# Linear attention's output kept by pairs of heads, with norm, factors and gates of each pair applied by PSUM bank

## The chip, the cores and the metric

The program runs on one core of a Trainium2 chip. Its engines are TensorE (PE, matrix products and transposes), VectorE (DVE), ScalarE (ACT) and GpSimd (POOL); SyncE (SP) issues the DMAs. The metric is the device time of one execution in microseconds, as the median of several runs. One profiled execution gives the trace from which all rows here are read.

## The reference, cut to what matters

One step of a hybrid decoder layer over 2048 prompt tokens and 32 sample tokens, all in float32. What the change touches is the mixer's linear attention (GLA) and what follows it up to the output projection:

```python
q, k, v, r, a, u, sv = split_cols(xn @ w_in)
logg = log_sigmoid(a @ w_alpha + b_alpha) / GLA_TAU
o, S = gla_chunked(q, k, v, logg, s0)          # S_t = diag(alpha_t) S_{t-1} + k_t^T v_t ; o_t = q_t S_t
o = rmsnorm(o, g_gla_out)                      # over the 128 values of each of 4 heads
o = o.reshape(B, T, GLA_WIDTH) * silu(r)
s_out = gelu(u) * sgu_spatial(rmsnorm(gelu(sv)), w_s, b_s)
y = concatenate([o, s_out]) @ w_out
```

Behind the mixer come a cross attention over 256 memory tokens, a gated feed-forward network with a short convolution, and the final norm. The program has all of them; the change leaves them alone.

## The kernel before

The prompt is worked in four blocks of 512 tokens (0 to 3); block 1 also carries the 32 sample tokens, so that its tiles are 544 wide. Large products are made of three matmuls of rounded parts (`mm3`, lines 92 to 94): each weight is split into `h_` and `l_` parts, each activation too. One block runs the input projection (tiles `t_wv`, `a_wu`, `t_wr`, ...), the linear attention, the spatial gating unit (`zp`, `z`), the output projection (`a_wo`), attention and the feed-forward network.

The linear attention works pair by pair (p is 0 or 1, two of the four heads each). For a pair, seven levels build the causal products in P: `e` (difference of sums, VectorE; two exponentials, ScalarE; times k, VectorE), `kr` (two on VectorE), four matmuls `s` (line 1044) into one PSUM bank, and two predicated copies of it into P (line 1048). Then `decay` and `states`: VectorE's `kh` (line 1073), its exponential on ScalarE (1079), its product with k on GpSimd (1080), four transposes `ktp` (1083), the copy `kt`, products `kv`, and the chain of states S. `chunks(p, i)` makes one PSUM bank `op` of 512 columns: two chunks of 128 tokens, two heads each; its two halves are copied to 256 columns of the tiles `o[c]`, one for each chunk of 128 tokens and 512 wide over all four heads.

When both pairs are in `o`, the tail runs: `onorm(c)` for each chunk (square on ScalarE, sum by heads on VectorE, `rt` on VectorE and `ors` on GpSimd for the inverse root, `o` times `r` on VectorE), `gate(c)` (`o` times `ors`), then `back(h)` for each head: four transposes `otp` (line 1185), one for each chunk, and the split into `ch` and `cl` that the output projection multiplies with.

What sets the order: `weave` lists the steps with the main work (input and output projections) and says between which main steps the others start; the framework's scheduler then lays the instructions out for each engine when the program is built, and each engine runs its own list in order, waiting on semaphores. So a step that moves in the list also moves work of other engines. In block 0 two fold stages of weights (`vop`, `voh`, `vol`) are woven in as well. `h_wo`, `l_wo`, `h_wr`, `l_wr` are splits of weights that arrive by DMA: ScalarE writes the `h_` part and VectorE the `l_` part.

## Time and profile before

| | us |
|---|---|
| median of 3 runs (lowest, highest) | 2838.52 (2836.45, 2841.78) |
| the profiled execution | 2836.71 |
| its span, first to last instruction | 2835.0 |
| TensorE busy in the span | 2794.4 (99%) |
| VectorE, ScalarE, GpSimd busy | 1891.3, 1104.5, 575.5 |
| TensorE's mean granted clock | 0.996 of full speed |

A row of the trace gives the start of an instruction or of a run of like instructions from the span's start, how long it lasted, engine, line, operation and tiles; in brackets stands the idle time of that engine ahead of it and the instruction that ended it. Matmuls are pipelined, so a row of one lasts longer than the distance to the next, and rates are read from distances. The granted clock is 1.00 at 2.4 GHz and 0.50 at 1.2 GHz.

### The profile page before, as it was taken

The numbers are of one execution on the slowest core, as the hardware profiler recorded it, in microseconds if no ns is written. First come the engines' busy times: TensorE is split into PE (matmuls) and PEld (weight loads), VectorE is DVE, ScalarE is ACT, GpSimd is POOL, SyncE is SP. The second block draws the span as 40 slices with busy tenths as digits, with TensorE's granted clock in tenths as the row PEclk, the third lists the DMA queues.
The fourth block names the chain that finished last, engine by engine and source line by source line (L and its number), as shares of the span: only waits on it lengthen the run. The fifth ranks groups of instructions, "written<-read, shape, count | busy, mean of one in ns | idle before, by whom it ended". The sixth has DMA issues, their size and how long they took to land.

```text
span 2835.0 us, 47063 instructions
## 1 busy us (share of the span) xinstructions
PE 2794.4 (99%) x17894; PEld 2473.9 (87%) x17894; DVE 1891.3 (67%) x3266; ACT 1104.5 (39%) x1950; POOL 575.5 (20%) x638
## 2 busy tenths in 40 slices
PE   8999999999999999999999999999999999999998
PEld 8888888888888898898888889899999888899997
DVE  6578778777657776655555777766666677665555
ACT  5645544333363354222124445422223545421222
POOL 2002212111111221222220121222221022132222
PEclk9999999999999999999999999999999999999999
DMA  9756589999932255888995226577776323577775
GB/s 306 244 182 219 188 273 340 335 339 333 328 109 77 83 164 196 309 290 290 324 340 169 82 61 208 196 260 256 258 264 215 102 70 133 201 260 273 271 282 177
DMA packets 369687, 638.21 MB, mean 225 GB/s; under 512 B 27370, under 2 KB 238412, under 8 KB 369462
## 3 DMA queue, kind: packets, MB, share of 16 engines
q1 hardware_dynamic: 369462, 635.20, 65.9%
q8 instruction: 142, 2.33, 0.3%
q14 instruction: 83, 0.68, 0.1%
HBM read 507.69 MB, written 127.41 MB: 224 GB/s over the span
## 4 chain that ended last, share of the span: by engine, by line
PE 61%; DVE 4%; ACT 1%; issue 1%; POOL 1%; DMA 0%; POOLq 0%; SPq 0%; DVEq 0%; ACTq 0%
PE d L94 4%; PE d L92 4%; PE d L93 4%; PE a_wx L94 1%; PE a_wx L93 1%; PE a_wx L92 1%; PE s L1044 1%; PE a_wo L92 1%; PE a_wo L93 1%; PE a_wu L92 1%; PE a_wu L93 1%; PE a_wo L94 1%; PE t_wr L92 1%; PE t_wr L93 1%; PE a_wu L94 1%
## 5 line engine op out<-in xcount | busy, mean ns | idle before, releaser
L92 PE MATMUL d<-acth,whi_wd 128*128 128x272 f32 (+1 forms) x688 | 235.3, 342 | 0.0
L94 PE MATMUL d<-acth,wlo_wd 128*128 128x272 f32 (+1 forms) x688 | 233.3, 340 | 0.0
L93 PE MATMUL d<-actl,whi_wd 128*128 128x272 f32 (+1 forms) x688 | 233.0, 339 | 0.0
L1679 DVE TENSOR_TENSOR h<-d,h 128x512 f32<-128x512 f32 (+1 forms) x232 | 133.5, 581 | 148.0 <-PE d L94 147.8
L1581 POOL TENSOR_TENSOR c<-c,bc_f 128x512 f32<-128x512 f32 (+1 forms) x88 | 139.3, 1589 | 134.2 <-ACT c L1580 133.4
L1571 ACT ACTIVATE c<-g,colsb 128x512 f32<-128x512 f32 x88 | 71.7, 815 | 202.9 <-DVE g L1540 152.7
L94 PEld LDWEIGHTS d<-acth,wlo_wd 128*128 128x128 f32 x688 | 129.3, 188 | 15.5 <-issue 1.2
L93 PEld LDWEIGHTS d<-actl,whi_wd 128*128 128x128 f32 x688 | 129.3, 188 | 13.6 <-issue 0.4
L92 PEld LDWEIGHTS d<-acth,whi_wd 128*128 128x128 f32 x688 | 129.5, 188 | 13.1
L1603 POOL TENSOR_TENSOR c<-r_q_wup,c 128x512 f32<-128x512 f32 (+1 forms) x33 | 63.0, 1908 | 337.7 <-DVE r_q_wup L286 215.9
L1568 POOL COPY carry<-g 128x2 f32<-128x2 f32 x88 | 30.6, 348 | 432.8 <-DVE g L1540 430.7
L92 PE MATMUL a_wo<-ch,h_wo 128*128 128x512 f32 (+1 forms) x320 | 113.2, 365 | 2.3 <-ACT r L874 1.5
L93 PE MATMUL a_wo<-cl,h_wo 128*128 128x512 f32 (+1 forms) x320 | 113.4, 357 | 0.0
L94 PE MATMUL a_wo<-ch,l_wo 128*128 128x512 f32 (+1 forms) x320 | 112.6, 355 | 0.0
L1572 DVE SCALAR_TENSOR_TENSOR c<-g,colsb,c 128x512 f32<-128x512 f32 x88 | 86.0, 978 | 29.0 <-ACT c L1571 28.3
L84 ACT ACTIVATE acth<-c 128x512 fp32r<-128x512 f32 (+1 forms) x88 | 55.9, 636 | 117.1 <-DVE c L1603 87.3
L94 PE MATMUL a_wx<-pTh,wlo_wx 128*128 128x512 f32 x256 | 101.2, 395 | 0.0
L93 PE MATMUL a_wx<-pTl,whi_wx 128*128 128x512 f32 x256 | 100.5, 393 | 0.0
L92 PE MATMUL a_wx<-pTh,whi_wx 128*128 128x512 f32 x256 | 100.2, 394 | 0.0
L1580 ACT ACTIVATE c<-c 128x512 f32<-128x512 f32 (+1 forms) x88 | 56.1, 637 | 96.6 <-DVE c L1573 84.7
L1573 DVE SCALAR_TENSOR_TENSOR c<-g,colsb,c 128x512 f32<-128x512 f32 x88 | 88.0, 1000 | 1.1
L85 DVE TENSOR_TENSOR actl<-c,acth 128x512 fp32r<-128x512 f32 (+1 forms) x88 | 64.2, 733 | 27.2 <-ACT acth L84 26.2
(3753 smaller groups left out, 9725.5 us busy)
## 6 DMA issues: line engine op xcount, KB each, us to landing
whi_wd<-wd SPq DMA_DIRECT2D x66, 512.0 KB, 7.8
wlo_wd<-wd SPq DMA_DIRECT2D x66, 512.0 KB, 7.5
r_wo<-in_w_out_dram SPq DMA_DIRECT2D x32, 512.0 KB, 3.5
...
```

Of the source, the lines that this page charges most:

```text
L84: act.activation(hi, src, AF.Copy)
L85: (lo_eng or dve).tensor_tensor(lo, src, hi.bitcast(F32), ALU.subtract)
L92: pe.matmul(ps, wh, xh, start=first, stop=False)
L93: pe.matmul(ps, wh, xl, start=False, stop=False)
L94: pe.matmul(ps, wl, xh, start=False, stop=last)
L1571: act.activation(c[:, :SB], g[:, 2:SB + 2], AF.Identity, bias=cb, scale=w2)
L1572: dve.scalar_tensor_tensor(c[:, :SB], g[:, 1:SB + 1], w1, c[:, :SB], ALU.mult, ALU.add)
L1573: dve.scalar_tensor_tensor(c[:, :SB], g[:, 0:SB], w0, c[:, :SB], ALU.mult, ALU.add)
L1580: act.activation(c[:, :T], c[:, :T], AF.Gelu_apprx_tanh)
L1581: pool.tensor_tensor(c[:, :T], c[:, :T], B.fbc[:, :T], ALU.mult)
L1603: (dve, pool)[i].tensor_tensor(c[:, :T], q[i], c[:, :T], ALU.mult)
L1679: dve.tensor_tensor(B.h[m + mm][:, cs], ps[:, :cw], B.h[m + mm][:, cs], ALU.add)
```

## The change

`B.o` is keyed by pair and bank, `o[p, i]`: one tile holds the 512 columns of one `op` bank.

- Pair 0: one copy of the whole bank (512 wide, in place of two of 256), the square from the copy, the sum by heads; the inverse root once for both banks (8 columns), and `gate(0, i)` directly behind. The factor `r` does not exist yet at that time; `times_r(0, i)` multiplies it in later, in the tail (two products 256 wide for each bank).
- Pair 1: no copy. ScalarE squares the PSUM bank itself, and VectorE's product with `r` reads the bank and writes `o` (`times_r(1, i, ps)`); then sum, inverse root and `gate(1, i)` by bank.
- The sample rows get the same by pair (`o[p, 2]`, 32x256).
- `states`, `chunks`, `smp` and the gates of pair 1 go to the tail's list, and the weave's numbers change.
- `back(h)` reads its four transposes from `o[p, c // 2]`.

```diff
-                B.o = [U(f"o{s}{c}") for c in range(nt)]
+                B.o = {}
+                B.oss, B.ors = narrow(f"oss{s}", 20), narrow(f"ors{s}", 20)
...
-                dve.tensor_copy(B.o[c][:, p * 256:(p + 1) * 256], ps[:, j * 256:(j + 1) * 256])
+            o, t = U(f"o{s}{p}{i}"), T_(f"osq{s}{p}{i}")
+            B.o[p, i] = o
+            if p == 0:
+                dve.tensor_copy(o[:, :512], ps)
+                act.activation(t[:, :512], o[:, :512], AF.Square)
+            else:
+                act.activation(t[:, :512], ps, AF.Square)
+                times_r(p, i, ps)
+            a = 8 * p + 4 * i
+            dve.tensor_reduce(B.oss[:, a:a + 4], t[:, :512].rearrange("p (h d) -> p h d", h=4), AX.X, ALU.add)
+            if p == 1:
+                rstd_of(B.ors[:, a:a + 4], B.oss[:, a:a + 4], 128, 4, 1.0 / 128)
+            elif i == 1:
+                rstd_of(B.ors[:, 0:8], B.oss[:, 0:8], 128, 8, 1.0 / 128)
+
+        def times_r(p, i, src):
+            for j in range(2):
+                js = slice(j * 256, (j + 1) * 256)
+                dve.tensor_tensor(B.o[p, i][:, js], src[:, js], B.r[2 * i + j][:, p * 256:(p + 1) * 256], ALU.mult)
...
-        def onorm(c):
-
-            if c == 0:
-                B.oss, B.ors = narrow(f"oss{s}", 20), narrow(f"ors{s}", 20)
-            n, hs = (128 if c < 4 else NS), slice(4 * c, 4 * c + 4)
-            t = T_(f"osq{s}{c}")
-            act.activation(t[:n, :512], B.o[c][:n, :512], AF.Square)
-            dve.tensor_reduce(B.oss[:n, hs], t[:n, :512].rearrange("p (h d) -> p h d", h=4), AX.X, ALU.add)
-            rstd_of(B.ors[:n, hs], B.oss[:n, hs], n, 4, 1.0 / 128)
-            dve.tensor_tensor(B.o[c][:n, :512], B.o[c][:n, :512], B.r[c][:n, :512], ALU.mult)
...
+        def gate(p, i):
+            n, nh, a = (128, 4, 8 * p + 4 * i) if i < 2 else (NS, 2, 16 + 2 * p)
+            o3 = B.o[p, i][:n, :nh * 128].rearrange("p (h d) -> p h d", h=nh)
+            dve.tensor_tensor(o3, o3, B.ors[:n, a:a + nh].unsqueeze(2).broadcast_to([n, nh, 128]), ALU.mult)
...
-                pe.transpose(ps[:, c * 128:(c + 1) * 128], B.o[c][:, hs_], ident)
+                a = (c % 2) * 256 + hh * 128
+                pe.transpose(ps[:, c * 128:(c + 1) * 128], B.o[p, c // 2][:, a:a + 128], ident)
...
+        def pair(p):
+            out = [lambda: states(p)] + [lambda i=i: chunks(p, i) for i in range(2)]
+            if sample:
+                out.append(lambda: smp(p))
+            return out + [lambda i=i: gate(p, i) for i in range(nt - 2)]
...
+        return [Step(f) for f in out], [Step(f) for f in pair(1) + [lambda i=i: times_r(0, i, B.o[0, i]) for i in range(2)] +
+                                        ([lambda: smp_r(0), lambda: smp_r(1)] if sample else []) +
+                                        [lambda h=h: back(h) for h in range(4)]]
...
-        steps += weave(proj + w1, *folds, (after, 0, 5), (sgu_st[:1], 6, 6), (sgu_st[1:nst], 11, 11), (sgu_st[nst:nst + 2], 12, 13), (sgu_st[nst + 2:], 16, 16), (gla[:1], 4, 4), (gla[1:2], 6, 6), (gla[2:12], 8, 10), (gla[12:-nlast], 10, 13), (gla[-nlast:], 16, 16), (gtail, 16, 18))
+        steps += weave(proj + w1, *folds, (after, 0, 5), (sgu_st[:1], 6, 6), (sgu_st[1:nst], 11, 11), (sgu_st[nst:nst + 2], 12, 13), (sgu_st[nst + 2:], 16, 16), (gla[:1], 4, 4), (gla[1:2], 6, 6), (gla[2:12], 8, 10), (gla[12:], 10, 13), (gtail, 16, 17))
```

The two programs hold the same matmuls and the same DMAs, and TensorE's order differs in four stretches, one in each block, from the second half of the linear attention to the output projection. VectorE has 8 instructions fewer, ScalarE 5 more (4 of them table loads), GpSimd 3 fewer.

TensorE at the end of block 3's linear attention, before: the last rows of output projection ahead of the transposes, and the first of sixteen `otp` in a row (tile numbers are the program's own; o_23881 and o_23882 are chunks 0 and 1).

```order
L92 MATMUL a_wo_24491<-ch_24364,h_wo_24153 128x512
L93 MATMUL a_wo_24491<-cl_24365,h_wo_24153 128x512
L94 MATMUL a_wo_24491<-ch_24364,l_wo_24154 128x512
L1185 MATMUL otp_24504<-ident,o_23881 128x128
L1185 MATMUL otp_24513<-ident,o_23881 128x128
L1185 MATMUL otp_24522<-ident,o_23881 128x128
L1185 MATMUL otp_24504<-ident,o_23882 128x128
L1185 MATMUL otp_24513<-ident,o_23882 128x128
```

And after: the rows around the transposes of pair 1's first bank (o_24396); those of the second bank (o_24414) stand seven `a_wo` further.

```order
L92 MATMUL a_wo_24433<-ch_24466,h_wo_24251 128x512
L93 MATMUL a_wo_24433<-cl_24467,h_wo_24251 128x512
L94 MATMUL a_wo_24433<-ch_24466,l_wo_24252 128x512
L92 MATMUL a_wo_24446<-ch_24466,h_wo_24251 128x512
L1203 MATMUL otp_24479<-ident,o_24396 128x128 x2
L1203 MATMUL otp_24488<-ident,o_24396 128x128 x2
L92 MATMUL a_wo_24433<-ch_24475,h_wo_24251 128x512
L93 MATMUL a_wo_24446<-cl_24467,h_wo_24251 128x512
L94 MATMUL a_wo_24446<-ch_24466,l_wo_24252 128x512
L92 MATMUL a_wo_24446<-ch_24475,h_wo_24251 128x512
L93 MATMUL a_wo_24433<-cl_24476,h_wo_24251 128x512
```

The sixteen transposes stood together; now those of pair 0 stand earlier, between other `a_wo`, and those of pair 1 in two groups of four with `a_wo` around them.

TensorE just ahead of the second `ktp` of block 3, before:

```order
L94 MATMUL t_wr_24171<-h_wr_24028,xl_7_23003 128x512
L1044 MATMUL s_24220<-kr_24216,e_24212 128x2x64 x4
L92 MATMUL t_wr_24178<-h_wr_24028,xh_6_22998 128x512
L93 MATMUL t_wr_24178<-l_wr_24029,xh_6_22998 128x512
L94 MATMUL t_wr_24178<-h_wr_24028,xl_6_22999 128x512
L92 MATMUL t_wr_24178<-h_wr_24028,xh_7_23002 128x512
L93 MATMUL t_wr_24178<-l_wr_24029,xh_7_23002 128x512
L94 MATMUL t_wr_24178<-h_wr_24028,xl_7_23003 128x512
L1083 MATMUL ktp_24239<-ident,kh_24235 128x128 x4
```

And after:

```order
L92 MATMUL t_wr_24181<-h_wr_24016,xh_7_22996 128x512
L93 MATMUL t_wr_24181<-l_wr_24017,xh_7_22996 128x512
L94 MATMUL t_wr_24181<-h_wr_24016,xl_7_22997 128x512
L1044 MATMUL s_24208<-kr_24204,e_24200 128x2x64 x4
L1044 MATMUL s_24223<-kr_24219,e_24215 128x2x64 x4
L1083 MATMUL ktp_24242<-ident,kh_24238 128x128 x4
```

Both last `s` groups (levels 5 and 6) stood among the `t_wr`, with nine and six of them behind; now they stand behind the last one, directly ahead of `ktp`. Counted from the second `zp` group to `ktp`, 43 `t_wr` stood in between and 30 do now; in block 0 it was 34 and is 17, in block 1 it was 46 (with levels 5 and 6) and is 36 (with levels 4, 5 and 6). In the order of ScalarE the split `h_wo` whose buffer the last `t_wr` matmuls still read stands ahead of the exponential of `kh` in blocks 1 to 3, where it stood behind it.

VectorE in block 0, level 6 and the first row of the decay, before:

```order
L1022 TENSOR_TENSOR e_2889<-b_2161 128x512
L85 TENSOR_TENSOR l_wo_2956<-r_wo_2953,h_wo_2955 128x1024
L1038 TENSOR_TENSOR e_2889<-e_2889,k_1759 128x4x64
L1034 SCALAR_TENSOR_TENSOR kr_2893<-e_2889,sel,q_1849 128x256 x2
L1073 TENSOR_TENSOR kh_2912<-b_2161 128x512
```

And after:

```order
L1022 TENSOR_TENSOR e_2898<-b_2161 128x512
L85 TENSOR_TENSOR l_wof_2993<-r_wof_2990,h_wof_2992 128x1024
L1038 TENSOR_TENSOR e_2898<-e_2898,k_1759 128x4x64
L1048 COPY_PREDICATED P_2606<-mask_141,s_2891 128x8x32
L1048 COPY_PREDICATED P_2611<-mask_141,s_2891 128x8x32
L1034 SCALAR_TENSOR_TENSOR kr_2902<-e_2898,sel,q_1849 128x256 x2
L1073 TENSOR_TENSOR kh_2921<-b_2161 128x512
```

The two predicated copies of level 5 (P with mask_141) moved ahead of level 6's `kr`, and so ahead of `kh`.

## Rows read from the trace of the kernel before

**Rows 1.** The page, busy time of each engine and the shares of the chain that ended last.

```profile
PE 2794.4 (99%) x17894; PEld 2473.9 (87%) x17894; DVE 1891.3 (67%) x3266; ACT 1104.5 (39%) x1950; POOL 575.5 (20%) x638
...
PE 61%; DVE 4%; ACT 1%; issue 1%; POOL 1%; DMA 0%; POOLq 0%; SPq 0%; DVEq 0%; ACTq 0%
```

**Rows 2.** The view of what TensorE waited for over the whole span: engine, transposed or multiplied tile and line, what ended the wait, then us in total, times, longest us.

```profile
PE otp L1185 <- DVE o L1179: 6.1, 3, 2.9
...
PE otp L1185 <- DVE vol L85: 2.2, 2, 1.3
...
PE ktp L1083 <- POOL kh L1080: 1.8, 1, 1.8
...
PE sc10S L92 <- DVE h L1238: 1.7, 1, 1.7
PE a_wo L92 <- ACT r L874: 1.5, 1, 1.5
...
PE a_wu L92 <- DVE u L856: 0.9, 1, 0.9
...
PE a_wo L92 <- ACT ch L88: 0.5, 1, 0.5
PE s L1044 <- ACT h_wof L84: 0.4, 1, 0.4
```

**Rows 3.** Busy time by stretch (windows): us from the span's start, length, then busy us and number of instructions of TensorE, of its weight loads, VectorE, ScalarE and GpSimd, then TensorE's granted clock as a share of full speed, the DMA share and GB/s.

```profile
1683.93:1690.75 6.82, 5.84 (x15) 4.47 (x16) 3.42 (x5) 2.42 (x4) 0.07 (x1) 0.50 0.26 79
2349.53:2356.35 6.82, 6.38 (x16) 4.84 (x17) 2.97 (x5) 2.43 (x4) 0.00 (x0) 0.50 0.19 66
1028.57:1031.98 3.41, 3.30 (x15) 3.01 (x15) 3.38 (x8) 3.41 (x7) 1.60 (x1) 0.50 0.03 12
252.00:257.00 5.00, 3.92 (x19) 3.32 (x20) 4.70 (x8) 1.06 (x2) 1.02 (x1) 1.00 0.17 50
286.00:292.00 6.00, 3.23 (x16) 2.27 (x17) 4.56 (x8) 2.82 (x6) 1.91 (x1) 1.00 1.01 358
```

**Rows 4.** Timeline, the end of the out projection's `otp` transposes in blocks 2 (first row) and 3: start us, us, engine, line, operation, out<-in, then in brackets the idle time ahead and what ended it.

```profile
1684.77 1.12 PE L1185 MATMUL otp<-ident,o 128*128 128x128 f32 x4 [2.88 <-DVE o L1179]
...
2349.08 0.69 DVE L1179 TENSOR_TENSOR o<-o,ors 128x512 f32<-128x512 f32 x1 [0.90 <-POOL ors L306]
...
2349.83 1.11 PE L1185 MATMUL otp<-ident,o 128*128 128x128 f32 x4 [2.77 <-DVE o L1179]
```

**Rows 5.** Timeline of TensorE in block 3, from the second `zp` group over 34 `t_wr` matmuls (first shown) to the first of the last two `s` groups; x8 is four matmuls with a record of each half.

```profile
2314.80 1.06 PE L914 MATMUL zp<-wsT,sv 128*128 128x128 f32 x8
2315.61 0.48 PE L94 MATMUL t_wr<-h_wr,xl 128*128 128x512 f32 x1
...
2323.58 1.06 PE L1044 MATMUL s<-kr,e 128*128 128x128 f32 x8
```

**Rows 6.** Timelines of block 0 between the second `zp` group and the second `ktp`: TensorE's two, then VectorE's rows of levels 5 and 6, the decay and the predicated copies, then the exponential and the product of `kh` on ScalarE and GpSimd.

```profile
239.92 1.06 PE L914 MATMUL zp<-wsT,sv 128*128 128x128 f32 x8
...
253.08 0.66 PE L1083 MATMUL ktp<-ident,kh 128*128 128x128 f32 x4 [1.83 <-POOL kh L1080]
...
245.20 1.90 DVE L1034 SCALAR_TENSOR_TENSOR kr<-e,sel,q 128x256 f32<-128x256 f32 x2
...
249.11 0.86 DVE L1034 SCALAR_TENSOR_TENSOR kr<-e,sel,q 128x256 f32<-128x256 f32 x2
...
250.50 1.39 DVE L1064 SCALAR_TENSOR_TENSOR qz<-q,sel,e 128x512 f32<-128x512 f32 x2
...
252.97 0.76 DVE L1048 COPY_PREDICATED P<-mask,s 128x256 f32<-128x256 uint8 x2
...
250.61 0.63 ACT L1079 ACTIVATE kh<-kh 128x512 f32<-128x512 f32 x1 [0.59 <-DVE kh L1073]
...
251.31 1.71 POOL L1080 TENSOR_TENSOR kh<-kh,k 128x512 f32<-128x512 f32 x1 [4.88 <-ACT kh L1079]
```

**Rows 7.** Timelines of block 1 at the same place: TensorE's first `s` group behind the second `zp`, and VectorE's `kr` of levels 5 and 6.

```profile
950.13 1.06 PE L1044 MATMUL s<-kr,e 128*128 128x128 f32 x8
...
945.30 0.87 DVE L1034 SCALAR_TENSOR_TENSOR kr<-e,sel,q 128x256 f32<-128x256 f32 x2
...
948.83 0.87 DVE L1034 SCALAR_TENSOR_TENSOR kr<-e,sel,q 128x256 f32<-128x256 f32 x2
```

**Rows 8.** Timelines of block 3, VectorE and GpSimd at levels 2 and 3 behind the first `zp` (where both run at once), a table load on ScalarE there, GpSimd's `kh`, and the `h_wo` split that waits for the last `t_wr`.

```profile
2301.95 2.31 DVE L85 TENSOR_TENSOR l_wo<-r_wo,h_wo 128x1024 fp32r<-128x1024 f32 x1
2304.19 1.51 DVE L1038 TENSOR_TENSOR e<-e,k 128x256 f32<-128x256 f32 x1
...
2306.41 0.68 DVE L1022 TENSOR_TENSOR e<-b 128x512 f32<-128x512 f32 x1
...
2301.57 1.61 POOL L927 TENSOR_TENSOR z<-z,u 128x512 f32<-128x512 f32 x1 [28.10 <-ACT u L857]
2304.08 1.33 POOL L85 TENSOR_TENSOR cl<-z,ch 128x512 fp32r<-128x512 f32 x1 [0.90 <-ACT ch L84]
...
2301.47 1.28 ACT L1024 ACT_TABLE_LOAD   x1
...
2324.22 1.53 POOL L1080 TENSOR_TENSOR kh<-kh,k 128x512 f32<-128x512 f32 x1 [3.60 <-ACT kh L1079]
...
2327.65 1.06 ACT L84 ACTIVATE h_wo<-r_wo 128x1024 fp32r<-128x1024 f32 x1 [3.50 <-PE t_wr L94]
```

More of the change, by code (lines that the diff above doesn't have):

```diff
@@ L1162, in smp, with smp_r @@
             pe.matmul(ps[:NS, :256], sum4, ot[:, :256], start=True, stop=True)
-            dve.tensor_copy(B.o[4][:NS, p * 256:(p + 1) * 256], ps[:NS, :256])
-        def onorm(c):
-            if c == 0:
-                B.oss, B.ors = narrow(f"oss{s}", 20), narrow(f"ors{s}", 20)
-            n, hs = (128 if c < 4 else NS), slice(4 * c, 4 * c + 4)
-            t = T_(f"osq{s}{c}")
-            act.activation(t[:n, :512], B.o[c][:n, :512], AF.Square)
-            dve.tensor_reduce(B.oss[:n, hs], t[:n, :512].rearrange("p (h d) -> p h d", h=4), AX.X, ALU.add)
-            rstd_of(B.ors[:n, hs], B.oss[:n, hs], n, 4, 1.0 / 128)
-            dve.tensor_tensor(B.o[c][:n, :512], B.o[c][:n, :512], B.r[c][:n, :512], ALU.mult)
-        def gate(c):
-            n = 128 if c < 4 else NS
-            o3 = B.o[c][:n, :512].rearrange("p (h d) -> p h d", h=4)
-            dve.tensor_tensor(o3, o3, B.ors[:n, 4 * c:4 * c + 4].unsqueeze(2).broadcast_to([n, 4, 128]), ALU.mult)
+            B.o[p, 2], t = U(f"o{s}{p}2"), T_(f"osq{s}{p}2")
+            dve.tensor_copy(B.o[p, 2][:NS, :256], ps[:NS, :256])
+            act.activation(t[:NS, :256], ps[:NS, :256], AF.Square)
+            a = slice(16 + 2 * p, 18 + 2 * p)
+            dve.tensor_reduce(B.oss[:NS, a], t[:NS, :256].rearrange("p (h d) -> p h d", h=2), AX.X, ALU.add)
+            rstd_of(B.ors[:NS, a], B.oss[:NS, a], NS, 2, 1.0 / 128)
+        def gate(p, i):
+            n, nh, a = (128, 4, 8 * p + 4 * i) if i < 2 else (NS, 2, 16 + 2 * p)
+            o3 = B.o[p, i][:n, :nh * 128].rearrange("p (h d) -> p h d", h=nh)
+            dve.tensor_tensor(o3, o3, B.ors[:n, a:a + nh].unsqueeze(2).broadcast_to([n, nh, 128]), ALU.mult)
+        def smp_r(p):
+            o = B.o[p, 2][:NS, :256]
+            dve.tensor_tensor(o, o, B.r[4][:NS, p * 256:(p + 1) * 256], ALU.mult)
         def back(h):
-            hs_ = slice(h * 128, (h + 1) * 128)
+            p, hh = divmod(h, 2)
             ps = mps(f"otp{s}{h}")
             for c in range(4):
-                pe.transpose(ps[:, c * 128:(c + 1) * 128], B.o[c][:, hs_], ident)
+                a = (c % 2) * 256 + hh * 128
+                pe.transpose(ps[:, c * 128:(c + 1) * 128], B.o[p, c // 2][:, a:a + 128], ident)
             hi, lo = U(f"ch{s}{h}", F32R), U(f"cl{s}{h}", F32R)
@@ L1189, in back @@
                 ps = mps(f"otps{s}{h}")
-                pe.transpose(ps[:, :NS], B.o[4][:NS, hs_], ident[:NS, :NS])
+                pe.transpose(ps[:, :NS], B.o[p, 2][:NS, hh * 128:(hh + 1) * 128], ident[:NS, :NS])
                 split_scaled(hi[:, SB:TM], lo[:, SB:TM], ps[:, :NS], gcol("ggla", h))
             B.cat[h] = (hi, lo)
+        def pair(p):
[3 more added lines that the diff above has]
+            return out + [lambda i=i: gate(p, i) for i in range(nt - 2)]
         out = [gates, lambda: cums(0)]
@@ L1200, in gla_steps @@
             out.append(lambda p=p: decay(p))
-            out += [lambda p=p: states(p)] + [lambda p=p, i=i: chunks(p, i) for i in range(2)]
-            if sample:
-                out.append(lambda p=p: smp(p))
-        tail = [lambda c=c: onorm(c) for c in range(nt)] + [lambda c=c: gate(c) for c in range(nt)]
-        tail += [lambda h=h: back(h) for h in range(4)]
-        return [Step(f) for f in out], [Step(f) for f in tail]
+            if p == 0:
+                out += pair(p)
+        return [Step(f) for f in out], [Step(f) for f in pair(1) + [lambda i=i: times_r(0, i, B.o[0, i]) for i in range(2)] +
+                                        ([lambda: smp_r(0), lambda: smp_r(1)] if sample else []) +
+                                        [lambda h=h: back(h) for h in range(4)]]
     def out_proj_steps(B, unit, src, g, name, sample, first, finished, keep=None, seven=False,
@@ L1759, in hymba_step_kernel @@
         gla, gtail = gla_steps(B)
-        nlast = 4 if B.mix_sample else 3
         sgu_st = sgu_steps(B)
```

## The prediction

> **What bounds the kernel now.** The page comes first: TensorE is busy for 2794 of 2835 us and its work is most of the chain that ended last [rows 1]. An edit that adds no matmul can therefore change only two things: the places where TensorE stands idle, and its clock. The view of what TensorE waited for lists both kinds of place that this change touches [rows 2]. The largest entry that is not a first load is the transposes of `o` waiting for the gates on VectorE: 6.1 us in three waits. Also there: the transposes of block 0 behind `vol`, the `ktp` transposes behind `kh` (1.8 us), and in block 1 `a_wo` behind `r` (1.5) and `a_wu` behind `u` (0.9). Then the granted clock in stretches: it is 0.50 for 6.82 us in each of blocks 2 and 3, beginning inside the wait for the transposes, and 1.00 around the waits of block 0 [rows 3]. So each long transpose wait is paid twice. All other stretches hold the same matmuls in the same order in both kernels and are not counted.
>
> **What is removed.** In blocks 2 and 3 the last four transposes wait 2.88 and 2.77 us for the last gate; the twelve transposes before them are done by then and nothing else stands there to cover the last `o` [rows 4]. Behind each wait come 6.82 us at half clock, of which 0.84 us (1684.77 less 1683.93) and 0.30 us lie in the wait itself; the rest is work at half speed, half of which is loss: 2.99 and 3.26 us [rows 3, 4]. After the change, the transposes of pair 0 are spread into the out projection; of those of pair 1 the first four stand 33 `a_wo` matmuls behind the last `op` and the other four seven later. At 0.234 us for one matmul of this size (34 `t_wr` from 2315.61 to 2323.58 [rows 5]) that is 7.7 us and 1.6 us more, and 0.5 for transposes between. VectorE has to do, for that last bank, two multiplies from the bank, a reduce, a `rt` and a gate, beside the same for the other bank, two `cl` and one `l_wo`. Its 512-wide gate takes 0.69 us [rows 4]; ten such and a split are 8 us, and the first four transposes need only the first bank's part of them. I take these waits as gone, with their half clock: 2.88 + 2.77 + 2.99 + 3.26 = **-11.9 us**. In block 0 the tail waits are 2.2 (`vol`) and 6.1 - 2.88 - 2.77 = 0.45 us (`o`); there too the matmuls of the fold now stand between the last `op` and the last transposes: **-2.65**. The wait for `ch` (0.5) stays, since a split still follows the last transpose.
>
> On what such a stretch costs there is a rule: by the Trainium skill (TensorE: Matmul & The Clock Gate, Terms) the penalty is about the throttled time times the part of the clock that is missing. That would be 3.4 us for each of these stretches, an estimate that makes this term 0.6 us larger; the rows give less, because part of the stretch is idle anyway.
>
> **What is moved: pair 1 is late at its `ktp`.** The early norm of pair 0 (two squares, two reduces, `rt`, two gates) now runs on VectorE and ScalarE between the pairs, and the levels of pair 1 come later. What no longer hides them is counted in matmuls: between `zp` and `ktp` 34 `t_wr` stand in block 0 before and 17 now; in block 3 43 before and 30 now, with both last `s` groups behind the last of them; in block 1 46 before, and 36 now with three levels in place of two. One `s` or `zp` group of four is 0.81 us (2314.80 to 2315.61 [rows 5]).
>
> Block 0. Let V be the end of `zp`, 239.92 + 0.81 = 240.73. VectorE's row of work from there to the `kr` of level 5 is the same in both (`vol`, `z`, `e`, `l_w`, `kr`), so that `kr` ends at V + 6.4 (245.20 + 1.90) [rows 6]. TensorE now gets there at V + 17 x 0.234 = V + 4.0: wait 2.4. The `kr` of level 6 ended at 249.98 before; two predicated copies of P now stand ahead of it (0.76, 0.67 net), so it ends at V + 9.9: wait 9.9 - 6.4 - 0.8 = 2.7. From that `kr` to `ktp` it was 253.08 - 249.98 = 3.1 us (`kh` on VectorE, ScalarE, then GpSimd [rows 6]); it is the same now, less 0.8 of `s`: wait 2.3. Sum 7.4 against 1.8 + 0.4 before [rows 2]: **+5.2**. Waits of 2.4, 2.7 and 2.3 us with little between them should draw the half clock as the 2.8 us waits did: **+3.0**.
>
> Block 1. `z` and the first level behind `zp` end their `kr` at 945.30 + 0.87 = 946.17, the second at 949.70 [rows 7]. These are now levels 4 and 5, the second later by part of an `l_wo` (0.6 to 1.1); level 6 needs `e`, two exponentials, a multiply and two `kr`, 2.55 us by the gap between such rows, and ends at 952.9 to 953.4. With the two copies of P ahead of `kh`, `ktp` follows 0.67 + 3.1 later, at 956.7 to 957.2. TensorE is there 36 x 0.234 + 3 x 0.81 = 10.85 us after 941.7 (the first `s` at 950.13 less the 36 `t_wr` ahead of it), at 952.6 [rows 5, 7]. Wait 4.1 to 4.6; the 1.55 for `r` goes, since `r` is ready by then: +2.8. `a_wu` behind `u` gives way to a wait for the sample row's copy, 0 to 1 us more, I take 0.3: **+3.1**. Its longest piece is about 3.0 us, so half clock again: **+3.0**.
>
> Blocks 2 and 3. Behind `zp`, VectorE does `z`, `e`, a split `l_wo`, `e` times `k`, `kr`, the next `e`, its product and `kr`. The split is new here, and VectorE is held while GpSimd works: `l_wo` took 2.31 us and ended 1.1 us after GpSimd's `z`, and the product 1.51 us with GpSimd's `cl` [rows 8]. From V on: `z` and `e` to 1.4, `l_wo` to 3.6, the product to 4.9 and `kr` to 5.7; the next `e` (0.68 us) to 6.3, its two exponentials to 7.1, product and `kr` to 8.3. TensorE has done 30 `t_wr` and one `s` at V + 7.8: wait 0.5. `ktp` comes 2.9 after that `kr` (GpSimd's `kh` takes 1.53 here), less 0.8 of `s`: 2.1, in all 2.6. The lower bound is a ScalarE matter: the `h_wo` split that waits for the last `t_wr` now stands ahead of the exponential of `kh`; 1.06 for it and 0.63 + 1.71 for `kh` on ScalarE and GpSimd, less two `s` groups, make 1.8 [rows 6, 8]. The upper is 3.0 (a GpSimd operation more in the way). I take 2.6, since the holds stand in rows: **+5.2** for both. Does a wait in pieces of 0.5 and 2.1 draw the half clock? One of 1.8 in block 0 did not, one of 1.7 in block 1 was followed by it, those of 2.8 did [rows 2, 3]. I count half of 3.1 for each: **+3.1**.
>
> Of waits behind a GpSimd operation there is also a rule. By the Trainium skill (SBUF — State Buffer, SBUF: two separate sides) whichever of VectorE with two SBUF inputs and GpSimd starts first keeps the shared port for the whole instruction, and the other blocks. That agrees with VectorE's held rows. It would also hold GpSimd's `kh` behind a `qz` of VectorE, up to 0.7 us in each block or 2.8 in all; the row shows `kh` starting at 251.31 while `qz` ran to 251.89 [rows 6], so the trace does not bear that half out, and the sum has none of it.
>
> **Off the path.** The squares from PSUM, the products with `r` from PSUM and the wider copies run on engines that wait most of the time; VectorE has 8 instructions fewer, ScalarE 5 more, four of them table loads at 1.28 us [rows 8]. In blocks 0, 2 and 3 two loads more stand between the pairs, ahead of level 1; the 13 `t_wr` (3 us) that were moved ahead of the second `zp` cover their 2.6 us. Without that cover, up to 1 us a block; 0 taken.
>
> **The sum.** -11.9 - 2.65 + 5.2 + 3.0 + 3.1 + 3.0 + 5.2 + 3.1 = +8.0 us. The profiled execution took 2836.7 (span 2835.0 and 1.7 around it), so 2844.7; the median of the three runs is 1.8 above it: 2846.
>
> **The rivals.**
> 1. *No half clock at the new waits.* What decides is whether activity between the pieces (an `s` group each) keeps the clock up; for it: block 0's tail has four waits in 4.5 us at clock 1.00 [rows 2, 3]. Against it: pieces of 2.3 to 3.0 us. Then 9.1 less: -1.1, 2837 to 2838, no measurable change.
> 2. *VectorE keeps ahead.* The levels reach it sooner than in my walk from V, because it waits less ahead of `zp`: the new waits shrink to their lower bounds (1.8 each in blocks 2 and 3, +3 in block 0, +1 in block 1) and nothing slows the clock. -14.55 + 3.6 + 3 + 1 = -7.0: 2831 to 2832. It decides when block 0's three waits sum to under 5 us.
> 3. *Half clock in all four blocks, and held GpSimd.* +3.1 for the two halves not counted, up to 2 for holds: 2851.
> 4. *The transposes still wait.* If VectorE reaches the last gate over 10 us after the last `op`, the removed 11.9 come back in part (2 us and half clock in each block): 2853 or more. Against it: the 8 us count.
>
> **How the numbers follow.** Forecast 0.40 (2841 to 2849), rival 1 0.26, rival 2 0.14, rival 3 0.15, rival 4 0.05. A measurement of this kernel can tell about 0.2%, 5.7 us, from no change. Slower by more (over 2844.2) holds rivals 3 and 4 and 0.32 of the forecast: 0.52; within it 0.08 + 0.26 = 0.34; faster 0.14. The range leaves out half of rival 2 and the top of rivals 3 and 4: 2833 to 2853.
>
> **What would show it.** In the changed kernel's list of TensorE's waits the `otp` rows behind `o` should be gone, and `ktp` behind `kh` should stand with some 10 us in four waits, with `s` behind `kr` for 6 to 8 us. The clock should be 1.00 in the out projections of blocks 2 and 3, and 0.50 for a stretch after the `ktp` of blocks 0 and 1. I am wrong in the mechanism if `ktp` waits under 1 us in blocks 2 and 3, or if `otp` still waits over 2 us there; wrong in size if the clock stays up in blocks 0 and 1.

## The result, and the profile after

| | before | after |
|---|---|---|
| median, us (lowest to highest, runs) | 2838.56 (2836.45 to 2844.42, 18) | 2846.59 (2840.83 to 2855.64, 18) |
| ratio to before (95% interval) | | 1.0026 (1.0018 to 1.0034) |
| span of the profiled execution | 2835.0 | 2845.0 |

The changed kernel is 8.0 us slower by the medians and 10.0 by the two spans. In single executions of the kernel before and of experiments 6 and 10 the clock is lower over the whole span; they are in none of the comparisons here.

The page of the changed kernel, busy times (compare [rows 1]):

```profile
PE 2798.4 (98%) x17894; PEld 2477.3 (87%) x17894; DVE 1891.7 (66%) x3258; ACT 1110.2 (39%) x1955; POOL 572.3 (20%) x635
```

The same matmuls are there, and VectorE has as much to do as before; the 10 us are a matter of when, not of how much. What TensorE waited for in the changed kernel (us in total, times, longest), beside [rows 2]:

```profile
PE ktp L1083 <- POOL kh L1080: 7.3, 4, 2.7
PE s L1044 <- DVE kr L1034: 5.7, 4, 2.4
...
PE s L1044 <- ACT h_wo L84: 1.7, 2, 0.9
...
PE opt L1181 <- DVE ot L1165: 1.4, 1, 1.4
...
PE sc20A L92 <- ACT w1wo L84: 0.9, 1, 0.9
...
PE sc30A L92 <- ACT w1wo L84: 0.7, 1, 0.7
PE sc20A L94 <- DVE w1wo L85: 0.7, 1, 0.7
PE sc30A L94 <- DVE w1wo L85: 0.7, 1, 0.7
```

No row of `otp` is left, and none of `a_wo` behind `r`. In their place stand four `ktp`, four `s` behind `kr`, and rows that the list before did not have: `s` behind the split `h_wo`, `opt` (a matmul of the sample rows in block 1), and the first score matmuls of the attention in blocks 2 and 3 (`sc20A`, `sc30A`).

The changed kernel's windows: us from the span's start, length, busy us (instructions) of TensorE, its weight loads, VectorE, ScalarE, GpSimd, then the granted clock, DMA share, GB/s. Beside [rows 3].

```profile
254.37:264.61 10.24, 8.13 (x25) 6.70 (x26) 6.18 (x11) 1.23 (x2) 1.71 (x1) 0.50 0.24 79
909.73:916.56 6.83, 6.83 (x33) 5.99 (x32) 5.42 (x13) 3.04 (x6) 4.86 (x4) 0.50 0.05 12
964.34:967.76 3.42, 3.42 (x19) 1.03 (x19) 3.42 (x9) 1.54 (x3) 0.00 (x0) 0.50 0.00 0
1670.00:1676.00 6.00, 3.70 (x25) 3.09 (x24) 5.52 (x11) 4.96 (x8) 1.71 (x1) 1.00 0.14 57
1684.00:1697.00 13.00, 13.00 (x74) 11.10 (x73) 8.19 (x15) 4.47 (x6) 4.19 (x4) 1.00 0.13 40
1827.91:1831.33 3.42, 3.42 (x18) 3.42 (x17) 2.57 (x9) 2.79 (x8) 1.90 (x3) 0.50 0.18 26
2336.00:2342.00 6.00, 3.66 (x26) 3.10 (x25) 5.51 (x11) 5.15 (x8) 1.71 (x1) 1.00 0.10 41
2350.00:2363.00 13.00, 13.00 (x73) 11.07 (x72) 8.00 (x15) 4.47 (x6) 4.00 (x3) 1.00 0.16 47
```

The out projections of blocks 2 and 3 (from 1684 and from 2350) now run without a gap at 1.00 (2.4 GHz); the 6.82 us at 0.50 in each are gone. Around the `ktp` of these blocks (1670 to 1676, 2336 to 2342) the clock stays at 1.00 although TensorE is busy for only 3.7 of 6 us. Half clock (0.50, 1.2 GHz) came in block 0, twice in block 1, and at the start of block 2's feed-forward network.

TensorE's timeline in block 0 of the changed kernel: the last `t_wr`, levels 5 and 6, the second `ktp` (compare [rows 6]):

```profile
249.29 0.40 PE L94 MATMUL t_wr<-h_wr,xl 128*128 128x512 f32 x1
252.04 1.13 PE L1044 MATMUL s<-kr,e 128*128 128x128 f32 x8 [2.35 <-DVE kr L1034]
255.57 2.05 PE L1044 MATMUL s<-kr,e 128*128 128x128 f32 x8 [2.40 <-DVE kr L1034]
258.52 1.11 PE L1083 MATMUL ktp<-ident,kh 128*128 128x128 f32 x4 [0.91 <-POOL kh L1080]
```

TensorE runs out of `t_wr` and then walks at VectorE's pace. VectorE's rows there, and GpSimd's `kh`:

```profile
251.02 0.87 DVE L1034 SCALAR_TENSOR_TENSOR kr<-e,sel,q 128x256 f32<-128x256 f32 x2
...
253.89 0.76 DVE L1048 COPY_PREDICATED P<-mask,s 128x256 f32<-128x256 uint8 x2
254.55 0.87 DVE L1034 SCALAR_TENSOR_TENSOR kr<-e,sel,q 128x256 f32<-128x256 f32 x2
...
256.76 1.71 POOL L1080 TENSOR_TENSOR kh<-kh,k 128x512 f32<-128x512 f32 x1 [5.94 <-ACT kh L1079]
```

Each `s` starts 0.15 us after its `kr` ends, and `ktp` right behind `kh` (256.76 + 1.71 = 258.47). The third wait is short mainly because the `s` ahead of it took 2.05 us in place of 1.06: it ran at half clock.

Block 3 of the changed kernel, TensorE from the second `zp` over 30 `t_wr` to `ktp`, then its transposes of pair 1 (compare [rows 4, 5]):

```profile
2329.10 1.06 PE L914 MATMUL zp<-wsT,sv 128*128 128x128 f32 x8
...
2338.53 1.13 PE L1044 MATMUL s<-kr,e 128*128 128x128 f32 x8 [0.51 <-DVE kr L1034]
2341.49 0.66 PE L1083 MATMUL ktp<-ident,kh 128*128 128x128 f32 x4 [1.84 <-POOL kh L1080]
...
2361.43 0.60 PE L1203 MATMUL otp<-ident,o 128*128 128x128 f32 x4
...
2363.48 0.60 PE L1203 MATMUL otp<-ident,o 128*128 128x128 f32 x4
```

VectorE, ScalarE and GpSimd there:

```profile
2334.16 1.91 DVE L1034 SCALAR_TENSOR_TENSOR kr<-e,sel,q 128x256 f32<-128x256 f32 x2
...
2358.94 0.69 DVE L1192 TENSOR_TENSOR o<-o,ors 128x512 f32<-128x512 f32 x1 [0.24 <-POOL ors L306]
...
2337.86 1.04 ACT L84 ACTIVATE h_wo<-r_wo 128x1024 fp32r<-128x1024 f32 x1
2339.01 0.63 ACT L1079 ACTIVATE kh<-kh 128x512 f32<-128x512 f32 x1
...
2333.86 1.54 POOL L85 TENSOR_TENSOR cl<-z,ch 128x512 fp32r<-128x512 f32 x1 [1.16 <-ACT ch L84]
```

The last gate ends at 2359.63, 1.8 us before the first transposes of that pair's heads, which therefore find `o` ready.

Two waits that stand elsewhere. Ahead of block 3's second `zp`, at level 2 of pair 1 (VectorE, ScalarE, GpSimd, TensorE):

```profile
2316.85 1.78 DVE L1022 TENSOR_TENSOR e<-b 128x512 f32<-128x512 f32 x1
...
2319.52 0.87 DVE L1034 SCALAR_TENSOR_TENSOR kr<-e,sel,q 128x256 f32<-128x256 f32 x2
...
2319.36 1.04 ACT L84 ACTIVATE h_wo<-r_wo 128x1024 fp32r<-128x1024 f32 x1
...
2316.59 1.49 POOL L85 TENSOR_TENSOR cl<-z,ch 128x512 fp32r<-128x512 f32 x1 [2.38 <-ACT ch L84]
...
2320.54 1.13 PE L1044 MATMUL s<-kr,e 128*128 128x128 f32 x8 [0.88 <-ACT h_wo L84]
```

The view puts this wait down to `h_wo`, which ended at 2320.40; but the `kr` that `s` reads ended at 2320.39, and `s` reads no `h_wo`. So this too is most likely an `s` behind `kr`: the level's `e` took 1.78 us in place of 0.68 while GpSimd's `cl` ran. In block 2 it is the same (1.78 us, wait 0.85).

In block 1, VectorE and then TensorE at the sample rows of pair 0:

```profile
908.40 0.68 DVE L1137 TENSOR_REDUCE oss<-osq 128x4 f32<-128x512 f32 x1
909.00 0.42 DVE L1165 COPY ot<-ops 128x256 f32<-128x256 f32 x1
...
909.47 0.84 PE L1181 MATMUL opt<-ot,sum 128*32 128x256 f32 x2 [1.37 <-DVE ot L1165]
```

`opt` waits for the copy `ot`, and directly ahead of `ot` stands a sum of pair 0's early norm.

**The books.** Waits of the changed kernel less those of before, and half of TensorE's busy time in each stretch at 0.50:

| place | counted | measured |
|---|---|---|
| tail waits of blocks 2 and 3, with their half clock | -11.9 | -2.88 - 2.77 - (5.84 + 6.38) / 2 = -11.8 |
| tail waits of block 0 | -2.65 | -2.6 |
| `a_wo` behind `ch`, block 0 | 0 | -0.45 |
| block 0: `s`, `s`, `ktp` | +5.2 | 2.35 + 2.40 + 0.91 - 1.83 - 0.36 = +3.5 |
| block 0: half clock | +3.0 | 8.13 / 2 = +4.1 |
| block 1: `ktp` and `opt`, less `r` and `u` | +3.1 | 2.73 + 1.37 - 1.55 - 0.88 = +1.7 |
| block 1: half clock (less that of before at 1028) | +3.0 | (6.83 + 3.42 - 3.30) / 2 = +3.5 |
| blocks 2 and 3: `s`, `ktp` | +5.2 | 0.47 + 1.83 + 0.51 + 1.84 = +4.7 |
| blocks 2 and 3: half clock there | +3.1 | 0 |
| level 2's `s`, blocks 2 and 3 | 0, of up to 1 a block | 0.85 + 0.88 = +1.7 |
| first scores, blocks 2 and 3 | not counted | 1.53 + 1.33 - 0.33 = +2.5 |
| first scores, block 1 | not counted | 1.01 + 0.64 + 0.63 + 0.51 + 0.65 - 1.69 - 0.82 = +0.9 |
| half clock at block 2's feed-forward network | not counted | 3.42 / 2 = +1.7 |
| sum | +8.0 | +9.4 |

The spans differ by 10.0. What is left, 0.6 us, is within the small waits at the start of the program (`mkt` behind `mkf` waits 2.6 us in place of 1.2, others there less than before).

### The profile page after: what moved, and what is told of

It reads as the page before. It is cut to its first block, busy times and chain, and to the rows that moved or that the text cites. A ratio compares the mean times of both kernels' runs of the same rounds, so it can differ in the third digit from the quotient of the medians.

```text
span 2845.0 us, 47058 instructions
## 1 busy us (share of the span) xinstructions
PE 2798.4 (98%) x17894; PEld 2477.3 (87%) x17894; DVE 1891.7 (66%) x3258; ACT 1110.2 (39%) x1955; POOL 572.3 (20%) x635
## 4 chain that ended last, share of the span: by engine, by line
PE 88%; DVE 5%; ACT 3%; DMA 2%; issue 1%; POOL 1%; SPq 0%; POOLq 0%; DVEq 0%; ACTq 0%
PE d L94 6%; PE d L92 6%; PE d L93 6%; PE a_wx L94 2%; PE a_wx L93 2%; PE a_wx L92 2%; PE a_wg L92 1%; PE a_wg L93 1%; PE a_wup L94 1%; PE a_wup L93 1%; PE a_wg L94 1%; PE a_wup L92 1%; PE a_wo L92 1%; PE a_wo L94 1%; PE a_wo L93 1%
```

## The experiments

The theory: the loss is made at the `s` and `ktp` of pair 1, because pair 0's early steps push pair 1's levels down the list, so that fewer `t_wr` matmuls stand between `zp` and `ktp` to cover VectorE's walk. Rivals: pair 0's early norm is itself the cost, as work of VectorE and ScalarE; GpSimd's `kh` in the chain is; or the products that read the PSUM bank are.

**1. Pair 0's square, sum, root and gates moved to the head of the tail.** All else as in the change.

```diff
-                act.activation(t[:, :512], o[:, :512], AF.Square)
...
+        def norm0(i):
+            t = T_(f"osq{s}0{i}")
+            act.activation(t[:, :512], B.o[0, i][:, :512], AF.Square)
...
-            return out + [lambda i=i: gate(p, i) for i in range(nt - 2)]
+            return out + ([lambda i=i: gate(p, i) for i in range(nt - 2)] if p else [])
...
+        first = [lambda i=i: norm0(i) for i in range(2)] + [lambda i=i: gate(0, i) for i in range(nt - 2)]
```

> Pair 0 only copies its bank early; its square, sum, inverse root and gates go to the head of the tail. Everything else as in the changed kernel. In the program's order the levels of pair 1 stand where they stood before the change (38 and 7 t_wr around level 6 in block 0, 44 t_wr between zp and ktp in blocks 2 and 3). Theory (the early norm of pair 0 pushes pair 1's levels late): the waits of s and ktp fall back to those of before (2 us in block 0, none in blocks 2 and 3, a_wo behind r 1.5 us in block 1), no half clock in block 0, and the transposes still do not wait: 2824 to 2831 us, faster than both. Rival A (reading the PSUM bank for square and product holds TensorE's banks): the time stays at 2843 or more. Rival B (VectorE can't do both norms in the tail): otp waits 2 to 3 us for o again in blocks 2 and 3, 2834 to 2841.

2823.4 us (2820.39 to 2825.52, 5 runs), ratio 0.994 (0.9926 to 0.9954), just below the range. TensorE in block 3 from the second `zp`:

```profile
2307.38 1.06 PE L914 MATMUL zp<-wsT,sv 128*128 128x128 f32 x8
2316.39 1.05 PE L1044 MATMUL s<-kr,e 128*128 128x128 f32 x8
2317.97 1.05 PE L1044 MATMUL s<-kr,e 128*128 128x128 f32 x8
2320.25 0.60 PE L1083 MATMUL ktp<-ident,kh 128*128 128x128 f32 x4
```

No brackets: 44 `t_wr` cover both levels and `kh`, and the transposes don't wait either. The waits of the transposes stay removed, and those of `s`, `ktp` and `opt` are gone; `a_wo` waits 1.25 us for `r` again.

**2. No work early, the list shifted by empty steps.** Experiment 1 with two empty steps (three in block 1) where the gates of pair 0 stood.

```diff
             if p == 0:
-                out += pair(p)
+                out += pair(p) + [lambda: None] * (nt - 2)
```

> The fastest kernel so far (pair 0's norm in the tail), with two empty steps in the list where the early gates stood (three in block 1): no instruction more, the levels of pair 1 only come later in the list. The order again has both last s groups directly ahead of ktp, with 33 t_wr behind zp in block 0, 32 in blocks 2 and 3, and block 1 as in the changed kernel. Theory (cover between zp and ktp decides, whoever takes it): waits return without any early work: 2 us in block 0 as before the change, 2.0 to 2.5 in each of blocks 2 and 3, some 4 with half clock in block 1: 2831 to 2836. Rival (VectorE's early instructions themselves cost): 2823 to 2826.

2831.3 us (2827.45 to 2833.36, 8 runs), ratio 0.9973 (0.9963 to 0.9983), at the low end of the range. TensorE's waits:

```profile
PE ktp L1083 <- POOL kh L1080: 7.6, 4, 2.7
...
PE s L1044 <- DVE kr L1034: 0.6, 1, 0.6
```

Steps that do nothing brought four `ktp` waits back (1.82, 2.74, 1.62 and 1.45 us), 2.7 us of first scores in blocks 2 and 3, and 7.9 us in all. The position in the list costs by itself; no added work is needed for it.

**3. The early work kept, the list started sooner.** The changed kernel, with pair 1's levels spread over main steps 10 to 12.

```diff
-... (gla[12:], 10, 13), (gtail, 16, 17))
+... (gla[12:], 10, 12), (gtail, 16, 17))
```

> The changed kernel, early norm and gates of pair 0 included, with only the weave's end for the second list changed from 13 to 12, so that pair 1's levels come one main step earlier. The order leaves 48 t_wr between zp and ktp in block 0 (17 in the changed kernel), 54 in blocks 2 and 3 (30), and nine t_wr behind the last s group in block 1; in blocks 0, 2 and 3 the last s group still stands directly ahead of ktp. Theory (cover between zp and ktp decides): the waits of s go, ktp keeps 1 to 2.2 us in blocks 0, 2 and 3, and the half clock of block 0 goes; 2828 to 2838. Rival (the early work of pair 0 itself costs the time): 2843 or more.

2826.07 us (2824.15 to 2830.31, 5 runs), ratio 0.9959 (0.9946 to 0.9971), better than expected. Block 3 again:

```profile
2303.03 1.06 PE L914 MATMUL zp<-wsT,sv 128*128 128x128 f32 x8
2313.65 1.05 PE L1044 MATMUL s<-kr,e 128*128 128x128 f32 x8
2315.23 1.05 PE L1044 MATMUL s<-kr,e 128*128 128x128 f32 x8
2318.22 1.05 PE L1044 MATMUL s<-kr,e 128*128 128x128 f32 x8
2319.10 0.65 PE L1083 MATMUL ktp<-ident,kh 128*128 128x128 f32 x4
```

The squares, sums, roots and gates of pair 0 all still run early, and nothing waits behind this `zp`: 54 `t_wr` stand there. What is left are `ktp` in block 0 (1.84 us) and an `s` just ahead of `zp` in blocks 2 and 3 (0.59 and 0.52). So the early work does not make the loss at `s` and `ktp`. It is not free, though: `opt` waits 1.36 us in block 1, with 3.41 us at 0.50 behind it. Every kernel with pair 0's sums early has this wait in its trace (1.36 to 1.46 us), and none with them in the tail. TensorE's order differs there too (in experiment 1 ten `a_wu` stand ahead of `opt`), so the shares of the two are not separated. This may be the 2.7 us by which experiment 3 stays behind experiment 1; the two intervals overlap.

**4. `kh` on VectorE.** The chain from `zp` to `ktp` then has one engine fewer.

```diff
-            pool.tensor_tensor(kh[:, :T], kh[:, :T], B.k[p][:, :T], ALU.mult)
+            dve.tensor_tensor(kh[:, :T], kh[:, :T], B.k[p][:, :T], ALU.mult)
```

> The product of kh with k runs on VectorE in place of GpSimd (0.7 us in place of 1.5 to 1.7). The order then leaves only 13 t_wr behind zp in blocks 2 and 3 (30 in the changed kernel) and 8 in block 0 (17). Theory (what counts is VectorE's walk from zp to ktp against the matmuls that stand there): the walk gets 0.9 us shorter and the cover 4.0 us (block 0: 2.1 us) shorter, so the waits of s and ktp grow to 5 to 6 us in each of blocks 2 and 3, with half clock behind them, and to 7 us in block 0: 2853 to 2862. Rival (GpSimd's slow product is what makes ktp late): the waits fall by 0.9 us in each block, 2840 to 2844.

2862.16 us (2860.54 to 2863.74), ratio 1.008 (1.0067 to 1.0092), at the top of the range. TensorE's waits:

```profile
PE s L1044 <- DVE kr L1034: 14.5, 6, 5.5
PE ktp L1083 <- DVE kh L1080: 8.5, 4, 4.2
```

The scheduler laid the program out anew and left only 13 `t_wr` behind `zp` in blocks 2 and 3. With less cover the loss is larger. The engine and the cover changed at once here, and 4.5 us are a wait that was not expected (`a_wu` behind `u` in block 1); that GpSimd's place in the chain is not the cause follows from experiments 1 and 3, where `kh` stays on GpSimd and the waits go.

**5. Only the gates of pair 0 listed in the tail.**

```diff
-            return out + [lambda i=i: gate(p, i) for i in range(nt - 2)]
+            return out + ([lambda i=i: gate(p, i) for i in range(nt - 2)] if p else [])
+        first = [lambda i=i: gate(0, i) for i in range(nt - 2)]
```

> Only the two gates of pair 0 go to the head of the tail; its squares, sums and roots stay early. In the order block 1's levels stand as before the change, but s of levels 5 and 6 still stand directly ahead of ktp in blocks 0, 2 and 3, with 18 and 23 t_wr behind zp. Theory: waits remain in blocks 0, 2 and 3 (7 us in block 0, 4 us each in 2 and 3, since 23 t_wr hide 1.6 us less than 30) and go in block 1; 2842 to 2848. Rival (the gates, not the place of the levels, are what costs): 2830 to 2836.

2848.64 us (2847.89 to 2851.24), ratio 1.0034 (1.0021 to 1.0046), just above the range. It did not test what it was meant to: the scheduler placed the two gates early on VectorE all the same. The `t_wr` behind `zp` fell to 23 in block 3, and `s` and `ktp` waited 1.82 and 2.30 us there.

**6. Squares, sums and roots early, gates behind the product with `r`.**

```diff
-... pair(1) + [lambda i=i: times_r(0, i, B.o[0, i]) for i in range(2)] + ...
+... pair(1) + [lambda i=i: (times_r(0, i, B.o[0, i]), gate(0, i)) for i in range(2)] + ...
```

> Pair 0's squares, sums and roots stay early, its gates stand behind the product with r, so they can't run before the tail. In the order block 1's levels stand as before the change, blocks 2 and 3 have 34 and 3 t_wr around the last two s groups, block 0 has 23 t_wr behind zp. Theory (each VectorE operation ahead of pair 1's levels takes cover from them; gates are half of the early work): waits of 5 us at s and ktp remain in block 0 with half clock, 1 to 2.5 us each in blocks 2 and 3, none in block 1 beyond a_wo behind r: 2829 to 2837, about half way between e1 (2823) and the changed kernel. Rival (early squares and sums with their table loads are what costs, not the gates): 2843 or more.

2835.17 us (median of 11), ratio 0.9988 (0.9978 to 0.9997), within the range. 37 `t_wr` stand behind `zp` in block 3 and `ktp` waits 0.63 us; the transposes wait again (0.81 and 0.82 us in blocks 2 and 3), since both gates of pair 0 now stand late.

These runs together, in block 3 (the count from TensorE's order, between the second `zp` and `ktp`; the waits of `s` and `ktp` in that stretch from each trace):

| kernel | `t_wr` as cover | waits, us |
|---|---|---|
| `kh` on VectorE | 13 | 0.88 + 3.48 + 1.54 = 5.90 |
| gates of pair 0 listed in the tail | 23 | 1.82 + 2.30 = 4.12 |
| the changed kernel | 30 | 0.51 + 1.84 = 2.35 |
| empty steps | 32 | 1.45 |
| gates behind `r` | 37 | 0.63 |
| before | 43 | 0 |
| norm of pair 0 in the tail | 44 | 0 |
| levels earlier | 54 | 0 |

The wait falls with every row until it is gone: from 13 to 43 matmuls, 30 x 0.234 = 7.0 us of cover, it falls by 5.9. Two rows are not quite like the others: with `kh` on VectorE the walk itself is shorter, and in the last row three levels stand behind `zp` in place of two.

**7 and 8. The bank of pair 1 copied first**, in the changed kernel and in experiment 1; square and product with `r` then read the copy.

```diff
-            if p == 0:
-                dve.tensor_copy(o[:, :512], ps)
-                act.activation(t[:, :512], o[:, :512], AF.Square)
-            else:
-                act.activation(t[:, :512], ps, AF.Square)
-                times_r(p, i, ps)
+            dve.tensor_copy(o[:, :512], ps)
+            act.activation(t[:, :512], o[:, :512], AF.Square)
+            if p == 1:
+                times_r(p, i, o)
```

> Pair 1's bank is copied to SBUF first, and square and product with r read the copy: 8 copies more on VectorE. The order up to ktp is that of the changed kernel. Theory (the waits sit ahead of ktp and have nothing to do with PSUM reads): same as the changed kernel within 3 us, 2844 to 2850, with the same waits of s and ktp. Rival A (reads of PSUM cost TensorE or VectorE): 2840 or less.

> The fastest kernel so far with pair 1's bank copied to SBUF ahead of square and product. Theory (reading the bank directly saves VectorE 0.7 us for each bank on the way to the last transposes, and shows only where that way is the last to arrive): waits of a_wo for ch of 0.5 us or of otp for o of up to 1 us in some blocks: 2824 to 2829. Rival (reads of PSUM in place of SBUF are a gain by themselves): 2830 or more. Third: no difference, 2821 to 2824.

2853.41 us (2852.55 to 2858.55), ratio 1.0051 (1.0038 to 1.0064): outside its range, on the slow side. With the norm in the tail 2827.0 (2824.49 to 2829.84), ratio 0.9959 (0.9947 to 0.9971), as expected. Copying costs 6.8 and 3.6 us against the same kernel without it; in the second case the two intervals overlap a little. In the first, `s` and `ktp` wait as long as in the changed kernel (5.7 and 7.3 us); what is new are `a_wo` behind `ch` (0.56 us in each of blocks 2 and 3), the first scores of block 0 (1.3), and 3.41 us at 0.50 at 1046 in block 1 (up to 1.6). So reading the bank directly is no part of the loss; it is faster than copying it first. Some 2.7 of the 6.8 us are not placed.

**9. Experiment 1 with the tail over main steps 16 to 18**, as before the change.

```diff
-... (gtail, 16, 17))
+... (gtail, 16, 18))
```

> The fastest kernel so far with the tail's steps spread over main steps 16 to 18 as before the change, in place of 16 and 17. The sixteen transposes stand together again in blocks 2 and 3, 28 a_wo behind the last op (8 before the change). Theory (the distance in matmuls from the last op to the last otp must cover VectorE's 8 us): 28 x 0.234 = 6.6 us leave a wait of 1 to 2 us in blocks 2 and 3, perhaps with half clock: 2825 to 2834. Rival (the form of the norm by banks alone removes the wait): 2822 to 2824.

2826.69 us (2823.39 to 2830.4), ratio 0.9961 (0.9947 to 0.9974). The expected `otp` waits did not come, and the interval overlaps that of experiment 1. Where the tail ends does not make the transposes late here. The sixteen stand together again, so that alone is not what made them wait before; they are 28 `a_wo` behind the last `op` in place of 8.

**10 and 11. Two useless matmuls in block 1's `ktp` bank**, ahead of the transposes that overwrite it, to fill the wait; run a second time for a trace of that stretch.

```diff
+            if p == 1 and s == 1:
+                for _ in range(2):
+                    pe.matmul(ps, ident, B.qz[2][:, :512], start=True, stop=True)
```

> The changed kernel with two useless matmuls of 512 columns in block 1 only, written into the ktp bank ahead of the four transposes that overwrite it; they read qz, which VectorE writes while GpSimd works on kh. The order is that of the changed kernel apart from these two. Theory (the half clock behind the ktp wait of block 1 comes from the idle 2.7 us, and it costs half of the work that runs in it): the wait before ktp splits into smaller ones with 1.6 us of work between, the granted clock stays 1.00 behind ktp, and the stretch from ktp to the end of block 1's output projection gets 1 to 1.7 us shorter; the whole time 2843 to 2847. Rival (the clock fell for another reason, the small matmuls of the sample rows ahead): half clock at the same place, no shorter.

> The same kernel as the one with two useless 512-column matmuls in block 1's ktp bank, for a trace that the first run of it did not give. If the 2.74 us wait of the changed kernel's ktp in block 1 is what drew the 3.4 us at half clock right behind it, the wait shrinks to about 1 us and the clock stays at 1.00 there, while the 6.8 us behind the opt wait stay as they are; the time is unchanged or up to 1 us lower. If the clock falls there for another reason, the 3.4 us at half clock stand behind the filled wait too. Time 2844 to 2848 in both cases.

2846.07 us (ratio 1.0022, 1.0012 to 1.0032) and 2846.36 (1.0023, 1.0014 to 1.0032), as the changed kernel. Windows of the second run's trace, behind `opt` and around `ktp`:

```profile
912.48:915.89 3.41, 3.41 (x17) 3.41 (x17) 3.41 (x7) 2.23 (x5) 2.79 (x3) 0.50 0.08 19
...
964.00:968.00 4.00, 3.94 (x32) 2.31 (x32) 4.00 (x11) 2.38 (x5) 0.00 (x0) 1.00 0.22 61
```

With the 2.73 us wait cut to 0.93 the clock is 1.00 behind `ktp`, where the changed kernel had 0.50. The three traces with a wait of 2.73 or 2.74 us there (the changed kernel, experiments 2 and 7) have 3.41 us at 0.50 that begin in it or right behind it, and this one has none there, so the idle time drew it, as far as four traces show it. The time is no shorter: in this trace 3.41 us at 0.50 stand at 1042, where the changed kernel has none. Behind the untouched `opt` wait the half clock stands as before, for a shorter time.

**12. Experiments 1 and 3 together.**

```diff
+        first = [lambda i=i: norm0(i) for i in range(2)] + [lambda i=i: gate(0, i) for i in range(nt - 2)]
...
+... (gla[12:], 10, 12), (gtail, 16, 17))
```

> Pair 0's square, sum, root and gates are listed at the head of the tail, and the second pair's levels over steps 10 to 12 in place of 10 to 13: both remedies at once. If the cover ahead of ktp is all that matters, nothing is left for the second remedy in blocks 0, 2 and 3, where the first left no wait of s, ktp or otp: 2821 to 2826, the same as either alone. If the earlier levels also take away what was left in block 1 (a_wo behind r 1.25 us, half clock 6.8 us), 2817 to 2820. A rival: 39 t_wr stand ahead of the second ktp already, and to start the levels sooner crowds VectorE ahead of zp; then 2826 to 2832 with new s waits.

2825.85 us (2823.67 to 2827.93, 6 runs), ratio 0.995 (0.9938 to 0.9961): within the first of its ranges, and no better than either. Both remedy the same loss; experiment 1, at 2823.4 us, is the fastest found, 15 us below before.

## Why the prediction came out as it did

The time was right: 2846 forecast, 2846.59 measured, slower by more than 0.2%. Its steps one by one:

- **The tail waits with their half clock, -11.9 and -2.65: right.** No `otp` waits; the clock is 1.00 in both out projections. The wait of `a_wo` for `ch` (0.45), which the text kept, went too. Experiments 1 and 2 lack these waits without an early norm, so it is not the early norm that removes them. The transposes' distance from the last `op` (33 `a_wo`, 28 in experiment 9, 8 before) or the norm by banks does; no run separates the two.
- **Fewer matmuls ahead of `ktp`: right, and shown** to be the cause of these waits by the table of cover, by the empty steps and by the earlier levels. In block 3 the walk from `zp` was forecast to put the two `kr` at V + 5.7 and V + 8.3; with V = 2329.91 they ended at V + 6.2 and V + 8.5. `kr` was held, 1.91 us in place of 0.87, while GpSimd's `cl` ran. The waits came to 2.3 and 2.35 us against 2.6.
- **Block 0, +5.2: over by 1.7.** The first two waits were right (2.35 and 2.40 for 2.4 and 2.7). The third was 0.91 and not 2.3: the sum put half clock behind the three waits, but it began between them, and the slower `s` filled part of the last wait.
- **Block 0's half clock, +3.0: there, and larger**, 10.24 us. By the Trainium skill (TensorE: Matmul & The Clock Gate, Terms) the penalty is about the throttled time times the missing half, 5.1 us as an estimate. The row has TensorE busy for 8.13 us of it, so some 4.1 could be lost.
- **Block 1, +3.1 and +3.0: near in sum (+5.2), wrong in parts.** `ktp` waited 2.73 and not 4.1 to 4.6, since VectorE came to the levels about 1 us earlier than the walk from before had it. The wait for the sample row's copy was seen: put at 0 to 1 us more than the 0.88 of `a_wu` and taken as 0.3, it was 0.5 more (`opt`, 1.37). Not seen was the half clock behind it, 6.83 us, twice as long as that behind `ktp`.
- **Half clock in blocks 2 and 3, +3.1 as half of two: this step failed.** The pieces of 0.5 and 1.84 left the clock at 1.00 in both blocks.
- **Put at nothing: late levels ahead of `zp`, +1.7 us.** The text gave up to 1 us a block for two more table loads ahead of level 1 and took 0. Level 1 came in time; level 2 did not, in blocks 2 and 3, where its `e` was held beside `cl`.
- **Not in the sum: +5.2 us.** The first scores of blocks 1 to 3, and a half clock at block 2's feed-forward network. The prediction took the stretches outside the one it read as the same; the first scores stand right behind it, and there TensorE now waits for splits. What made these late, and why the clock fell at the feed-forward network (TensorE waits 0.26 us there in both kernels), no run shows.

So the mechanism at `ktp` was right, and the closeness of the number was luck: terms that came out lower than forecast (block 0's waits, block 1's `ktp`, the clock of blocks 2 and 3 above all) make 7.3 us, terms that were too small 1.7, and those put at nothing or left out 6.9. Of the signs that the text named, the `otp` rows went and the clock did as said; `ktp` waits 7.3 us and not some 10, `s` behind `kr` 5.7 and not 6 to 8. Rival 1 (no half clock at the new waits) held for blocks 2 and 3 and fell for blocks 0 and 1. Rival 2 had the right condition for block 0 (three waits over 5 us decide against it: they were 5.66). Rivals 3 and 4 fell.
